# Hybrid attention block on one core: last value tiles and lambda moved, weight differences on VectorE, row scalings placed behind sums

## The chip, the cores and the metric

The kernel runs on one core of one Trainium2 chip. A time is the device time of one execution in microseconds (us); the number for a kernel is the median of several executions. One execution is recorded by the hardware profiler, and every row of a profile below is from that one.

Engines have short names in the profile: PE is TensorE's matrix products and PEld its weight loads (which overlap products), DVE is VectorE, ACT is ScalarE, POOL is GpSimd, SP is SyncE, which here only issues transfers.

## The reference

One decoder block on a sequence of 1024 rows of width 1024, all in float32. Every product is kept near float32 accuracy by splitting operands, as told in the next section.

```
h    = rms_norm(x, g_pre)
proj = h @ w_in                       # qa ka va fa za | qb kb vb zb | gates
ya   = fox_attention(qa, ka, va, log_sigmoid(fa + b_forget)) * silu(za)  # 8 heads of 64
qd, kd = rope(qb), rope(kb)           # 4 heads, two maps (q1,k1), (q2,k2) each
lam  = exp(sum(lambda_q1*lambda_k1)) - exp(sum(lambda_q2*lambda_k2)) + lam_init
yb   = (softmax(q1 k1^T) - lam * softmax(q2 k2^T)) v     # causal
yb   = rms_norm(yb, g_subln) * (1 - lam_init) * silu(zb)
ga, gb = sigmoid(gates)
merged = ga * (ya @ w_branch[0]) + gb * (yb @ w_branch[1])
out  = x + rms_norm(merged @ w_out, g_post)
```

## The kernel before, in words

**Split operands.** A float32 operand is held as `hi`, its rounding to the type fp32r, and `lo`, the remainder. A product of two operands is three products on PE: hi by hi, hi by lo, lo by hi. So each operand costs a copy (`hi`, on ACT or GpSimd) and a subtraction (`lo`, mostly on VectorE). For projection weights `load_w` does that (L260 the load, L264 or L266 `hi`, L268 `lo`), in three rings of slots with the tags `wraw`, `whi`, `wlo` of the pool `wpool`, two slots each. A tile that takes a slot waits until all readers of the tile two before it in that ring are done, stores to memory among them.

**Value phase (to about 111 us).** `x_block` normalises 128 rows of x and transposes them on PE (`xt`) into `hT`. `v_block(i)`, for eight row blocks, multiplies them with the value weights (`pv`, L197), splits the result into `vbs{i}` (values of the differential heads) and `vas{i}` (those of the forgetting heads), which are stored to memory as `vb_d` and `va_d` on SP's queue (L205, L213). `vbs` lies in the ring `whi`, `vas` in the ring `wlo`: the rings that `load_w` uses for the first keys' and queries' weights afterwards. Between blocks `h_combinations(k)` makes the sums of blocks of `hT` that the gates need later and stores them (`t_d`), through the four slots of the ring `wvraw` of the pool `xp`.

**Units 0 to 7 (about 111 to 582 us).** Units 0 to 3 are the differential heads, 4 to 7 pairs of forgetting heads. For each: keys and queries are projected (`pk`, `pq`, L278), in units 0 to 3 rotated: ACT copies the projection (`rawk`, L315), four transfers on SP bring its quarters into swapped order (`swk`, L319), VectorE multiplies by the cosines (L321), GpSimd the swapped tile by the sines (L322), VectorE adds (L323). Then come logits (`Sd`, `Sf`), softmax, and the products with the values. Lambda (`nlam`) is computed ahead of unit 0, in a tile `lt` of the pool of the softmax tiles: four small loads on SP (L588), two products (L591) and two sums (L593) on VectorE, an exponential on ACT, two small operations on VectorE (L596, L597).

**Gates (about 582 to 739 us) and branches (739 to 826 us).** The gate products and, at the end, the output products run by a scheme of seven products of half blocks instead of eight (`wino`, L728 the sums of its results on VectorE, L735 its products on PE, `x1` to `x7`). Its left operands are made in `left_operands`: sums `S1` to `S4` of blocks (L699), split into `a1` to `a7` (L686 `hi` on ACT, L687 `lo` on VectorE or GpSimd). In the branch stage, `branch` multiplies with `w_branch` (`pb`, L869), and `merge` multiplies by the stored gate on VectorE (L882, straight from PSUM, which frees the bank for PE; there are eight) and, for the second branch, adds to the merged tile `mg` on GpSimd (L884).

**Output weights.** Beside the branch products the seven right operands of the output products are made from the four blocks of `w_out`: `wo_sub` (L917) makes differences of 128x1024 on GpSimd, in place; `wo_parts` splits them (L910 on ACT, L911 on VectorE). The last of them and the first output operands are made side by side at about 826 to 840 us.

**Output (about 826 us to the end).** Four pairs of row blocks (i, i+4), named `o0` to `o3`, with seven products of 12 matmuls each. When the sum of a half row is done, `out_half` squares it on ACT (L965) and multiplies it by the output norm's weights (L968); when both halves of a row are there, ACT adds the two sums of squares (`ors`, L980) and GpSimd takes the power (L981). `row_out` then scales the two halves and adds the residual x (L997) and stores them. The residual loads (L947) go into columns of `mg` that are no longer needed. A generator step of `wino` is one product with its sums; `advance` runs one step, then issues the `row_out` that became ready in the step before:

```
        due = waiting[:]
        waiting.clear()
        next(gen, None)
        for f in due:
            f()
```

**What sets the order.** The program is written in one sequence; a scheduler with a simulated timeline then sets the order in which each engine's instructions stand, by its own costs and by when tiles come free. A changed dependence in one place can so change the order elsewhere. On each engine and each queue, instructions run strictly in that order. `tc.issue_after(ins)` tells the scheduler to place what is issued within it behind `ins`.

Of the kernel before, what the change touches and what calls it, by code (L numbers as in the profile page):

```python
# [16 lines left out]
P = 128  # L17
# [30 lines left out]
def tile_hybrid_block(  # L48
# [72 lines left out]
    with ExitStack() as st:  # L121
# [63 lines left out]
        def v_block(i):  # L185
            sl = slice(i * P, (i + 1) * P)
            hs = slice(i % 4 * P, (i % 4 + 1) * P)
            chunks = ((0, 512), (512, 768), (768, 1032))
            ps = [
                pv1.tile([P, CH], F32, tag=f"v{n}", name=f"pv{i}_{n}")[:, 0:b - a]  # L190
                for n, (a, b) in enumerate(chunks)
            ]
            for n, (a, b) in enumerate(chunks):
                first = True
                for k in range(KT):
                    for hp, wt in ((0, wv_hi), (0, wv_lo), (1, wv_hi)):
                        nc.tensor.matmul(  # L197
                            ps[n], lhsT=hT[hp][k // 4][i // 4][:, k % 4, hs], rhs=wt[k][:, a:b],
                            start=first, stop=(k == KT - 1 and hp == 1))
                        first = False  # L200
            sb = wpool.tile([P, 4, 256], F32R, tag="whi", name=f"vbs{i}")
            p0 = ps[0].rearrange("p (h c) -> p h c", h=4)
            nc.scalar.copy(sb[:, :, 0:128], p0)
            nc.vector.tensor_tensor(sb[:, :, 128:256], p0, sb[:, :, 0:128], op=ALU.subtract)
            nc.sync.dma_start(vb_d[sl], f32(sb))  # L205
            sa = wpool.tile([P, 8, 128], F32R, tag="wlo", name=f"vas{i}")
            for n, hh in ((1, 0), (2, 4)):
                pa = ps[n][:, 0:256].rearrange("p (h c) -> p h c", h=4)
                nc.scalar.copy(sa[:, hh:hh + 4, 0:64], pa)
                nc.vector.tensor_tensor(  # L210
                    sa[:, hh:hh + 4, 64:128], pa, sa[:, hh:hh + 4, 0:64], op=ALU.subtract)
            nc.vector.tensor_tensor(fg[:, i, :], ps[2][:, 256:264], bf_bc, op=ALU.add)
            nc.sync.dma_start(va_d[sl].rearrange("s a (b c) -> s (a b) c", b=2), f32(sa))  # L213

        def h_combinations(k):
# [24 lines left out]
            nc.vector.tensor_tensor(f21, f21, f11, op=ALU.subtract)  # L240
            parts(4, f21)

        x_block(0)
        for k in range(KT):
            load_wv(k)
# [3 lines left out]
        for i in range(NB):  # L249
            for j in XBLK[i]:  # L250
                x_block(j)
            v_block(i)
            for k in TBLK[i]:
                h_combinations(k)

# [27 lines left out]
    with ExitStack() as st:  # L283
# [299 lines left out]
            return load, load_v, groups  # L583


        lt = pp.tile([P, 4, 64], F32, tag="P", name="lt")
        for n, v in enumerate((lq1, lk1, lq2, lk2)):
            nc.sync.dma_start(lt[:, n, :], v[0:1].to_broadcast([P, 64]))  # L588
        le = small.tile([P, 2], F32, tag="le", name="le", bufs=1)
        for n in range(2):  # L590
            nc.vector.tensor_tensor(  # L591
                lt[:, 2 * n, :], lt[:, 2 * n, :], lt[:, 2 * n + 1, :], op=ALU.mult)
            nc.vector.tensor_reduce(  # L593
                out=le[:, n:n + 1], in_=lt[:, 2 * n, :], axis=mybir.AxisListType.X, op=ALU.add)
        nc.scalar.activation(le, le, AF.Exp)
        nc.vector.tensor_tensor(nlam, le[:, 1:2], le[:, 0:1], op=ALU.subtract)  # L596
        nc.vector.tensor_scalar(nlam, nlam, -LAM_INIT, None, op0=ALU.add)  # L597

        def forget_sums():

            fgf = fg.rearrange("p a b -> p (a b)")
# [89 lines left out]
    def left_operands(nm, a11, a12, a21, a22):  # L691
# [24 lines left out]
            return t  # L716
        return get

    def wino(nm, left, right, order, out11, out12, out21, out22):

        x, c = {}, {}
# [3 lines left out]
            return c[key]  # L725

        def add(dst, a, b):
            nc.vector.tensor_tensor(dst, a, b, op=ALU.add)  # L728

        for m in order:  # L730
            a = left(m)
# [142 lines left out]
    def merge(d, br, c, ps):  # L874
        sl = slice(c * CH, (c + 1) * CH)
        m = mg[:, d, sl]
        if br == 0:
            g = m
        else:
            g = tmp.tile([P, CH], F32, tag="t", name=f"gb{d}_{c}")  # L880
        nc.sync.dma_start(g, g_d[d][br][:, sl])
        nc.vector.tensor_tensor(g, ps, g, op=ALU.mult)  # L882
        if br == 1:
            nc.gpsimd.tensor_tensor(m, m, g, op=ALU.add)  # L884

    for br in range(2):
        for d in range(KT):
# [26 lines left out]
    def wo_sub(dst, a, b):  # L914
        for j in range(2):
            js = slice(2 * j, 2 * j + 2)
            nc.gpsimd.tensor_tensor(dst[:, js], a[:, js], b[:, js], op=ALU.subtract)  # L917

    wo_parts(1, r[1, 1], hslot[1, 1])
    wo_sub(r[1, 1], r[1, 2], r[1, 1])  # L920
# [26 lines left out]
        nc.sync.dma_start(xs, x2[i * P:(i + 1) * P, :].rearrange("p (k n) -> p k n", k=KT))  # L947
        xres[i] = xs

    waiting = []  # L950

    def advance(gen):

        due = waiting[:]
        waiting.clear()
        next(gen, None)
        for f in due:
            f()

    def out_half(i, e, o, st):  # L960

# [16 lines left out]
        if len(st) == 2:  # L978
            rs = small.tile([P, 1], F32, tag="ors", name=f"ors{i}")
            nc.scalar.activation(rs, ss, AF.Identity, bias=st[0][2])  # L980
            nc.gpsimd.tensor_tensor(rs, rs, mhalf[:, 0:1], op=ALU.pow)  # L981
            if i not in xres:
                residual(i, i)
            waiting.append(lambda: row_out(i, rs, st))

    def row_out(i, rs, st):
        for n, (e, o, _) in enumerate(st):
# [32 lines left out]
    for n, which in enumerate((0, 0, 0, 0, 0, 1, 0, 0, 1, 1, 1, 1, 1, 1)):  # L1020
        advance(pairs[which])
        if n == 0:
            for i in (3, 7):
                residual(i, i - 2)
    for f in waiting:
        f()
    xst.close()
    gw.close()
# [42 lines left out]
```

## Time and profile before

| what | us |
|---|---|
| median of three executions | 918.48 (919.04, 915.05, 918.48) |
| the profiled execution | 915.13 |
| its span, first to last instruction | 913.4 |
| PE busy | 885.6 (97%) |
| PE weight loads busy | 746.7 (82%) |
| VectorE busy | 604.2 (66%) |
| GpSimd busy | 468.5 (51%) |
| ScalarE busy | 440.5 (48%) |
| moved by DMA | 139.04 MB |

The mean granted clock of TensorE was 0.998 of full speed. A profile row that lists an instruction begins with its start and its duration in us, then the engine (SPq is SP's queue), the line of the kernel, the operation, output<-inputs without their numbers, the shapes, how many of them stand in the row, and in brackets how long the engine stood idle before it and what ended that idle time. A row of waits gives the instruction that waited, the one it waited for, and three numbers: us in total, times, the longest. A row of stretches gives the stretch, its length, the busy time of each engine and the count of its instructions, the granted clock, the DMA engines' busy share, and GB/s.

### The profile page before, as it was taken

To read this page: it belongs to the slowest core of one execution; us is meant where nothing else is said; L and a number is where in the kernel's file an instruction comes from. 1 tells how busy PE (TensorE), PEld (TensorE's weight loads), DVE (VectorE), ACT (ScalarE), POOL (GpSimd) and SP (SyncE) were. 2 spreads that over 40 slices of the span, in tenths; PEclk is the share of its full clock that TensorE was granted. 3 is DMA by queue.
4 is the path that set the end of the run, shared out by engine and by line. 5 is a ranking of instruction groups with operands and counts; after the bars stand their busy time and mean duration, and the time that the engine had idled before them with its cause. 6 is when DMAs were issued, how large, how long until landed. Compare 5 with 4: busy or idle time off the path is not lost. (4 is left out here: it accounts for less than half of the span.)

```text
span 913.4 us, 13656 instructions
## 1 busy us (share of the span) xinstructions
PE 885.6 (97%) x4600; PEld 746.7 (82%) x4600; DVE 604.2 (66%) x1123; ACT 440.5 (48%) x877; POOL 468.5 (51%) x439
## 2 busy tenths in 40 slices
PE   7999999999999999999999999999999999999996
PEld 5899978788888888888888888788888888887884
DVE  6757547878578574467648548425778893548996
ACT  3433225576657674365546648533443361313442
POOL 7325324545545456254434446417566526687861
PEclk9999999999999999999999999999999999999999
DMA  9556737434335260432523432596555498210395
GB/s 316 192 170 255 262 106 210 111 79 122 108 81 171 73 179 18 141 92 70 165 73 87 129 102 62 197 401 218 168 181 171 155 333 291 70 46 21 95 183 186
DMA packets 128648, 139.04 MB, mean 152 GB/s; under 512 B 10289, under 2 KB 96305, under 8 KB 127554
## 3 DMA queue, kind: packets, MB, share of 16 engines
q1 hardware_dynamic: 124210, 135.82, 47.4%
q0 software_dynamic: 4224, 2.10, 2.0%
q8 instruction: 36, 0.59, 0.3%
q14 instruction: 34, 0.28, 0.1%
q10 hardware_dynamic: 144, 0.26, 0.1%
HBM read 85.65 MB, written 37.81 MB: 135 GB/s over the span
## 5 line engine op out<-in xcount | busy, mean ns | idle before, releaser
L197 PE MATMUL pv<-wvhi,hT 128*128 128x264 f32 (+2 forms) x384 | 89.1, 324 | 0.4 <-DVE hT L183 0.4
L278 PE MATMUL pz<-hT,hi_z 128*128 128x512 f32 x256 | 83.3, 397 | 0.2 <-ACT sq L390 0.2
L278 PE MATMUL pk<-hT,hi_k 128*128 128x512 f32 x256 | 82.2, 395 | 0.9 <-DVE KB L331 0.9
L278 PE MATMUL pq<-hT,hi_q 128*128 128x512 f32 x256 | 81.7, 393 | 0.0
L735 PE MATMUL x_o<-wo_op,a_o 128*128 128x512 f32 x336 | 77.8, 392 | 1.1 <-ACT a_o L686 1.1
L869 PE MATMUL pb<-yT,hi_br 128*128 128x512 f32 x256 | 78.5, 389 | 0.0
L735 PE MATMUL x_g<-T,a_g 128*128 128x512 f32 x336 | 78.1, 391 | 0.0
L735 PEld LDWEIGHTS x_o<-wo_op,a_o 128*128 128x128 f32 x336 | 62.9, 188 | 15.8 <-ACT a_o L686 2.0
L735 PEld LDWEIGHTS x_g<-T,a_g 128*128 128x128 f32 x336 | 63.1, 188 | 13.9
L197 PEld LDWEIGHTS pv<-wvhi,hT 128*128 128x128 f32 x384 | 64.4, 190 | 6.1 <-DVE hT L183 0.7
L440 ACT ACTIVATE Pd<-Pd,mxd 128x128 f32<-128x128 f32 (+7 forms) x64 | 49.6, 775 | 35.4 <-DVE mxd L434 35.1
L553 POOL TENSOR_TENSOR cb<-cb,trim 128x128 f32<-128x128 f32 x64 | 30.3, 477 | 66.9 <-DVE mxf L434 44.1
L527 POOL TENSOR_SCALAR Pd<-Pd,l,nlam 128x128 f32<-128x128 f32 (+7 forms) x32 | 29.3, 915 | 65.6 <-DVE l L526 59.4
L197 PE MATMUL pv<-wvlo,hT 128*128 128x512 f32 (+2 forms) x192 | 62.1, 326 | 0.1
L558 POOL TENSOR_SCALAR Pf<-Pf,lf 128x1024 f32<-128x1024 f32 (+3 forms) x64 | 47.9, 753 | 27.7 <-DVE lf L557 24.7
L465 DVE TENSOR_TENSOR plf<-ptf,phf 128x512 fp32r<-128x512 f32 (+1 forms) x80 | 49.9, 635 | 18.0 <-ACT phf L464 17.2
L440 ACT ACTIVATE Pf<-Pf,mxf 128x1024 f32<-128x1024 f32 (+3 forms) x64 | 49.8, 777 | 20.6 <-DVE mxf L434 20.0
L735 PE MATMUL x_g<-hT,a_g 128*128 128x512 f32 x252 | 59.0, 391 | 0.0
L869 PEld LDWEIGHTS pb<-yT,hi_br 128*128 128x128 f32 x256 | 48.1, 188 | 9.9
L735 PEld LDWEIGHTS x_g<-hT,a_g 128*128 128x128 f32 x252 | 47.3, 188 | 10.4
L278 PEld LDWEIGHTS pk<-hT,hi_k 128*128 128x128 f32 x256 | 47.2, 188 | 10.3 <-DVE KB L331 1.5
L278 PEld LDWEIGHTS pq<-hT,hi_q 128*128 128x128 f32 x256 | 47.6, 188 | 9.2
(252 smaller groups left out, 2382.3 us busy)
## 6 DMA issues: line engine op xcount, KB each, us to landing
t_d<-t SPq DMA_DIRECT2D x16, 512.0 KB, 4.7
T<-t_d SPq DMA_DIRECT2D x8, 1024.0 KB, 17.8
raw<-in_w_in_dram SPq DMA_DIRECT2D x14, 512.0 KB, 5.5
vb_d<-vbs SPq DMA_DIRECT2D x8, 512.0 KB, 3.7
va_d<-vas SPq DMA_DIRECT2D x8, 512.0 KB, 3.1
raw_k<-in_w_in_dram SPq DMA_DIRECT2D x8, 512.0 KB, 5.0
raw_q<-in_w_in_dram SPq DMA_DIRECT2D x8, 512.0 KB, 4.4
V<-vb_d SPq DMA_DIRECT2D x4, 1024.0 KB
```

The costliest lines, as they stand in the source:

```text
L197: nc.tensor.matmul(ps[n], lhsT=hT[hp][k // 4][i // 4][:, k % 4, hs], rhs=wt[k][:, a:b], start=first, stop=(k == KT - 1 and hp == 1))
L278: nc.tensor.matmul(ps, lhsT=a[:, k, :], rhs=hT[h][k // 4][c][:, k % 4, :], start=(k == 0 and a is hi and h == 0), stop=(k == KT - 1 and a ...
L440: nc.scalar.activation(pr[:, 0:n], pr[:, 0:n], AF.Exp, bias=mx[:, len(pcs) - 1:len(pcs)], scale=-1.0, accum_out=le)
L465: nc.vector.tensor_tensor(pl[:, 0:n], pt[:, 0:n], ph[:, 0:n], op=ALU.subtract)
L527: nc.gpsimd.tensor_scalar(p2[:, 0:n], p2[:, 0:n], l2, nlam, op0=ALU.mult, op1=ALU.mult)
L553: nc.gpsimd.tensor_tensor(diag, diag, trim, op=ALU.add)
L558: nc.gpsimd.tensor_scalar(p1[:, 0:n], p1[:, 0:n], l1, 1.0, op0=ALU.mult, op1=ALU.mult)
L735: nc.tensor.matmul(x[m], lhsT=a[:, ai, k, :], rhs=right[m][bi][k], start=(k == 0 and n == 0), stop=(k == 3 and n == 2))
L869: nc.tensor.matmul(ps, lhsT=a[:, kk, :], rhs=yT[g][h][:, k % 2, sl], start=(k == 0 and a is hi and h == 0), stop=(k == 3 and a is lo))
```

## The change

Four edits; the arithmetic stays what it was.

- The value tiles of the last row block, `vbs7` and `vas7`, are taken from the ring `wvraw` of the pool `xp` (four slots) and not from `whi` and `wlo`.
- Lambda is computed in a function `lambdas()` that is called behind the third value block (i = 2) and not ahead of unit 0; its tile `lt` now comes from the ring `wlo`.
- `wo_sub` runs on VectorE and not on GpSimd, and so do the two last sums of `merge` (those of d = 7).
- `advance` holds each `row_out` for a number of steps (two for row 6, one for the others) and issues it behind the last sum made so far, by explicit order.

```diff
@@ -198,12 +198,15 @@
                             ps[n], lhsT=hT[hp][k // 4][i // 4][:, k % 4, hs], rhs=wt[k][:, a:b],
                             start=first, stop=(k == KT - 1 and hp == 1))
                         first = False
-            sb = wpool.tile([P, 4, 256], F32R, tag="whi", name=f"vbs{i}")
+            last = i == NB - 1
+            sb = (xp.tile([P, 4, 256], F32R, tag="wvraw", name=f"vbs{i}", bufs=4) if last
+                  else wpool.tile([P, 4, 256], F32R, tag="whi", name=f"vbs{i}"))
             p0 = ps[0].rearrange("p (h c) -> p h c", h=4)
             nc.scalar.copy(sb[:, :, 0:128], p0)
             nc.vector.tensor_tensor(sb[:, :, 128:256], p0, sb[:, :, 0:128], op=ALU.subtract)
             nc.sync.dma_start(vb_d[sl], f32(sb))
-            sa = wpool.tile([P, 8, 128], F32R, tag="wlo", name=f"vas{i}")
+            sa = (xp.tile([P, 8, 128], F32R, tag="wvraw", name=f"vas{i}", bufs=4) if last
+                  else wpool.tile([P, 8, 128], F32R, tag="wlo", name=f"vas{i}"))
             for n, hh in ((1, 0), (2, 4)):
                 pa = ps[n][:, 0:256].rearrange("p (h c) -> p h c", h=4)
                 nc.scalar.copy(sa[:, hh:hh + 4, 0:64], pa)
@@ -240,6 +243,21 @@
             nc.vector.tensor_tensor(f21, f21, f11, op=ALU.subtract)
             parts(4, f21)
 
+        def lambdas():
+
+            lt = wpool.tile([P, 4, 64], F32, tag="wlo", name="lt")
+            for n, v in enumerate((lq1, lk1, lq2, lk2)):
+                nc.sync.dma_start(lt[:, n, :], v[0:1].to_broadcast([P, 64]))
+            le = small.tile([P, 2], F32, tag="le", name="le", bufs=1)
+            for n in range(2):
+                nc.vector.tensor_tensor(
+                    lt[:, 2 * n, :], lt[:, 2 * n, :], lt[:, 2 * n + 1, :], op=ALU.mult)
+                nc.vector.tensor_reduce(
+                    out=le[:, n:n + 1], in_=lt[:, 2 * n, :], axis=mybir.AxisListType.X, op=ALU.add)
+            nc.scalar.activation(le, le, AF.Exp)
+            nc.vector.tensor_tensor(nlam, le[:, 1:2], le[:, 0:1], op=ALU.subtract)
+            nc.vector.tensor_scalar(nlam, nlam, -LAM_INIT, None, op0=ALU.add)
+
         x_block(0)
         for k in range(KT):
             load_wv(k)
@@ -250,6 +268,8 @@
             for j in XBLK[i]:
                 x_block(j)
             v_block(i)
+            if i == 2:
+                lambdas()
             for k in TBLK[i]:
                 h_combinations(k)
 
@@ -582,19 +602,6 @@
                                 u == 7 and g in FING)))
             return load, load_v, groups
 
-
-        lt = pp.tile([P, 4, 64], F32, tag="P", name="lt")
-        for n, v in enumerate((lq1, lk1, lq2, lk2)):
-            nc.sync.dma_start(lt[:, n, :], v[0:1].to_broadcast([P, 64]))
-        le = small.tile([P, 2], F32, tag="le", name="le", bufs=1)
-        for n in range(2):
-            nc.vector.tensor_tensor(
-                lt[:, 2 * n, :], lt[:, 2 * n, :], lt[:, 2 * n + 1, :], op=ALU.mult)
-            nc.vector.tensor_reduce(
-                out=le[:, n:n + 1], in_=lt[:, 2 * n, :], axis=mybir.AxisListType.X, op=ALU.add)
-        nc.scalar.activation(le, le, AF.Exp)
-        nc.vector.tensor_tensor(nlam, le[:, 1:2], le[:, 0:1], op=ALU.subtract)
-        nc.vector.tensor_scalar(nlam, nlam, -LAM_INIT, None, op0=ALU.add)
 
         def forget_sums():
 
@@ -716,6 +723,8 @@
             return t
         return get
 
+    sums = [None]
+
     def wino(nm, left, right, order, out11, out12, out21, out22):
 
         x, c = {}, {}
@@ -725,7 +734,7 @@
             return c[key]
 
         def add(dst, a, b):
-            nc.vector.tensor_tensor(dst, a, b, op=ALU.add)
+            sums[0] = nc.vector.tensor_tensor(dst, a, b, op=ALU.add).ins
 
         for m in order:
             a = left(m)
@@ -881,7 +890,8 @@
         nc.sync.dma_start(g, g_d[d][br][:, sl])
         nc.vector.tensor_tensor(g, ps, g, op=ALU.mult)
         if br == 1:
-            nc.gpsimd.tensor_tensor(m, m, g, op=ALU.add)
+            eng = nc.vector if d == KT - 1 else nc.gpsimd
+            eng.tensor_tensor(m, m, g, op=ALU.add)
 
     for br in range(2):
         for d in range(KT):
@@ -914,7 +924,7 @@
     def wo_sub(dst, a, b):
         for j in range(2):
             js = slice(2 * j, 2 * j + 2)
-            nc.gpsimd.tensor_tensor(dst[:, js], a[:, js], b[:, js], op=ALU.subtract)
+            nc.vector.tensor_tensor(dst[:, js], a[:, js], b[:, js], op=ALU.subtract)
 
     wo_parts(1, r[1, 1], hslot[1, 1])
     wo_sub(r[1, 1], r[1, 2], r[1, 1])
@@ -947,15 +957,15 @@
         nc.sync.dma_start(xs, x2[i * P:(i + 1) * P, :].rearrange("p (k n) -> p k n", k=KT))
         xres[i] = xs
 
-    waiting = []
+    waiting, step = [], [0]
 
     def advance(gen):
 
-        due = waiting[:]
-        waiting.clear()
+        step[0] += 1
         next(gen, None)
-        for f in due:
-            f()
+        while waiting and waiting[0][0] <= step[0]:
+            with tc.issue_after(sums[0]):
+                waiting.pop(0)[1]()
 
     def out_half(i, e, o, st):
 
@@ -981,7 +991,7 @@
             nc.gpsimd.tensor_tensor(rs, rs, mhalf[:, 0:1], op=ALU.pow)
             if i not in xres:
                 residual(i, i)
-            waiting.append(lambda: row_out(i, rs, st))
+            waiting.append((step[0] + (2 if i == 6 else 1), lambda: row_out(i, rs, st)))
 
     def row_out(i, rs, st):
         for n, (e, o, _) in enumerate(st):
@@ -1022,7 +1032,7 @@
         if n == 0:
             for i in (3, 7):
                 residual(i, i - 2)
-    for f in waiting:
+    for _, f in waiting:
         f()
     xst.close()
     gw.close()
```

How the order moves, at three places. Names in the rows are tiles with their serial numbers. The first place is VectorE at the end of the value phase; `lo_k0` and `lo_q0` are the remainders of the first keys' and queries' weights, `t6_3` and `t4_3` those of the last stored combinations of `hT`, `fg` the forget gates. Before:

```order
L204 TENSOR_TENSOR vbs7_1214<-pv7_0_1139,vbs7_1214 128x4x128
L268 TENSOR_TENSOR lo_k0_1282<-raw_k0_1279,hi_k0_1281 128x1024
L591 TENSOR_TENSOR lt_1262<-lt_1262 128x64
L210 TENSOR_TENSOR vas7_1218<-pv7_1_1140,vas7_1218 128x4x64
L593 TENSOR_REDUCE le_1267<-lt_1262 128x1
L591 TENSOR_TENSOR lt_1262<-lt_1262 128x64
L593 TENSOR_REDUCE le_1267<-lt_1262 128x1
L210 TENSOR_TENSOR vas7_1218<-pv7_2_1141,vas7_1218 128x4x64
L212 TENSOR_TENSOR fg_86<-pv7_2_1141,bf_bc_83 128x8
L596 TENSOR_TENSOR nlam_85<-le_1267 128x1
L597 TENSOR_SCALAR nlam_85<-nlam_85 128x1
L268 TENSOR_TENSOR lo_q0_1328<-raw_q0_1325,hi_q0_1327 128x1024
```

With the change:

```order
L288 TENSOR_TENSOR lo_k0_1282<-raw_k0_1279,hi_k0_1281 128x1024
L213 TENSOR_TENSOR vas6_1119<-pv6_1_1041,vas6_1119 128x4x64
L230 TENSOR_TENSOR t6_3_1142<-fa_3_1126,t6_3_1142 128x512
L213 TENSOR_TENSOR vas6_1119<-pv6_2_1042,vas6_1119 128x4x64
L215 TENSOR_TENSOR fg_86<-pv6_2_1042,bf_bc_83 128x8
L230 TENSOR_TENSOR t4_3_1148<-fb_3_1127,t4_3_1148 128x512
L206 TENSOR_TENSOR vbs7_1227<-pv7_0_1152,vbs7_1227 128x4x128
L288 TENSOR_TENSOR lo_q0_1328<-raw_q0_1325,hi_q0_1327 128x1024
L213 TENSOR_TENSOR vas7_1231<-pv7_1_1153,vas7_1231 128x4x64
L213 TENSOR_TENSOR vas7_1231<-pv7_2_1154,vas7_1231 128x4x64
L215 TENSOR_TENSOR fg_86<-pv7_2_1154,bf_bc_83 128x8
```

`lo_q0` now stands ahead of the two remainders of `vas7` and not behind them, `lo_k0` ahead of those of `vas6`, and lambda's operations are gone from here.

The second place is VectorE at the change from the branch stage to the output products; `wo_op61` and `wo_op41` are remainders of output weights, `wo11` and `wo21` the blocks in which the differences are made, `a5_o0` and `a6_o0` remainders of left operands of the first output pair. Before:

```order
L882 TENSOR_TENSOR gb7_1_8642<-pb7_1_1_8629,gb7_1_8642 128x512
L911 TENSOR_TENSOR wo_op61_8679<-wo11_8646,wo_op60_8678 128x1024
L911 TENSOR_TENSOR wo_op41_8687<-wo11_8646,wo_op40_8686 128x1024
L699 TENSOR_TENSOR S1_o0_8780<-mg_8053 128x512
L699 TENSOR_TENSOR S2_o0_8782<-S1_o0_8780,mg_8053 128x512
L699 TENSOR_TENSOR S1_o1_8802<-mg_8053 128x512
L687 TENSOR_TENSOR a5_o0_8824<-S1_o0_8780,a5_o0_8824 128x512
L699 TENSOR_TENSOR S2_o1_8804<-S1_o1_8802,mg_8053 128x512
L911 TENSOR_TENSOR wo_op41_8687<-wo11_8646,wo_op40_8686 128x1024
L687 TENSOR_TENSOR a6_o0_8784<-S2_o0_8782,a6_o0_8784 128x512
```

With the change:

```order
L921 TENSOR_TENSOR wo_op61_8679<-wo11_8646,wo_op60_8678 128x1024
L927 TENSOR_TENSOR wo11_8646<-wo21_8652,wo11_8646 128x1024
L894 TENSOR_TENSOR mg_8053<-mg_8053,gb7_1_8642 128x512
L927 TENSOR_TENSOR wo11_8646<-wo21_8652,wo11_8646 128x1024
L706 TENSOR_TENSOR S1_o0_8780<-mg_8053 128x512
L921 TENSOR_TENSOR wo_op41_8687<-wo11_8646,wo_op40_8686 128x1024
L706 TENSOR_TENSOR S2_o0_8782<-S1_o0_8780,mg_8053 128x512
L706 TENSOR_TENSOR S1_o1_8802<-mg_8053 128x512
L921 TENSOR_TENSOR wo_op41_8687<-wo11_8646,wo_op40_8686 128x1024
L694 TENSOR_TENSOR a5_o0_8824<-S1_o0_8780,a5_o0_8824 128x512
L706 TENSOR_TENSOR S2_o1_8804<-S1_o1_8802,mg_8053 128x512
L694 TENSOR_TENSOR a6_o0_8784<-S2_o0_8782,a6_o0_8784 128x512
```

The last two differences (L927) and the last merge sum (L894) now stand ahead of the sums `S1` and `S2`, and both `wo_op41` ahead of `a5_o0`. On PE, at the same place, the products of `x6_o0` and its neighbours stood so before:

```order
L735 MATMUL x7_o1_8767<-wo_op70_8664,a7_o1_8764 128x512
L735 MATMUL x6_o0_8787<-wo_op60_8678,a6_o0_8784 128x512
L735 MATMUL x6_o0_8787<-wo_op61_8679,a6_o0_8784 128x512
L735 MATMUL x6_o1_8809<-wo_op60_8678,a6_o1_8806 128x512
L735 MATMUL x6_o1_8809<-wo_op61_8679,a6_o1_8806 128x512
L735 MATMUL x5_o0_8827<-wo_op50_8670,a5_o0_8824 128x512
L735 MATMUL x5_o0_8827<-wo_op51_8671,a5_o0_8824 128x512
```

With the change:

```order
L744 MATMUL x7_o1_8767<-wo_op70_8664,a7_o1_8764 128x512
L744 MATMUL x6_o0_8787<-wo_op60_8678,a6_o0_8784 128x512
L744 MATMUL x6_o0_8787<-wo_op61_8679,a6_o0_8784 128x512
L744 MATMUL x6_o0_8787<-wo_op60_8678,a6_o0_8784 128x512 x2
L744 MATMUL x6_o0_8787<-wo_op61_8679,a6_o0_8784 128x512
...
L744 MATMUL x6_o0_8787<-wo_op60_8678,a6_o0_8784 128x512
L744 MATMUL x6_o1_8809<-wo_op60_8678,a6_o1_8806 128x512
L744 MATMUL x6_o1_8809<-wo_op61_8679,a6_o1_8806 128x512
L744 MATMUL x5_o0_8827<-wo_op50_8670,a5_o0_8824 128x512
```

All twelve products of `x6_o0` now follow each other; before, those of two more products stood behind its first two, and its last ten behind `x4_o0`'s first.

The third place is VectorE at the end; `c12_o3` and `c11_o3` are the sums for row 3, `go7` and `go3` rows 7 and 3. Before:

```order
L728 TENSOR_TENSOR cu2_o3_9226<-x4_o3_9279,cu2_o3_9226 128x512
L968 TENSOR_TENSOR go7_0_9295<-cu2_o3_9226,gx_8705 128x512
L997 SCALAR_TENSOR_TENSOR go7_1_9273<-go7_1_9273,ors7_9297,mg_8053 128x512
L997 SCALAR_TENSOR_TENSOR go7_0_9295<-go7_0_9295,ors7_9297,mg_8053 128x512
L728 TENSOR_TENSOR c12_o3_9248<-x3_o3_9305,c12_o3_9248 128x512
L968 TENSOR_TENSOR go3_1_9321<-c12_o3_9248,gx_8705 128x512
L728 TENSOR_TENSOR c11_o3_9150<-x2_o3_9331,c11_o3_9150 128x512
```

With the change:

```order
L737 TENSOR_TENSOR cu2_o3_9226<-x4_o3_9279,cu2_o3_9226 128x512
L978 TENSOR_TENSOR go7_0_9295<-cu2_o3_9226,gx_8705 128x512
L737 TENSOR_TENSOR c12_o3_9244<-x3_o3_9305,c12_o3_9244 128x512
L1007 SCALAR_TENSOR_TENSOR go7_1_9273<-go7_1_9273,ors7_9297,mg_8053 128x512
L1007 SCALAR_TENSOR_TENSOR go7_0_9295<-go7_0_9295,ors7_9297,mg_8053 128x512
L978 TENSOR_TENSOR go3_1_9321<-c12_o3_9244,gx_8705 128x512
L737 TENSOR_TENSOR c11_o3_9150<-x2_o3_9331,c11_o3_9150 128x512
```

The sum `c12_o3` moved ahead of the two scalings of row 7.

## The prediction, made before the changed kernel was run

> **What bounds the kernel now.** I read the page's busy shares first, then what TensorE (PE) waits for, then the stretches round those waits.
>
> ```profile
> PE 885.6 (97%) x4600; PEld 746.7 (82%) x4600; DVE 604.2 (66%) x1123; ACT 440.5 (48%) x877; POOL 468.5 (51%) x439
> ```
>
> PE is busy for 885.6 of 913.4 us, so what can be saved without taking products away is the 28 us in which it stands still. Its waits name part of them:
>
> ```profile
> PE Sd L432 <- DVE mxd L434: 3.2, 5, 1.2
> PE pq L278 <- DVE lo_q L268: 1.8, 1, 1.8
> PE x_o L735 <- ACT a_o L686: 1.1, 2, 0.8
> ```
>
> The change reaches two of them: `pq` waiting for the first query weights' remainder `lo_q`, and `x_o`, the output products, waiting for an operand. (The three numbers are us in total, times, longest.) The third place is the stretch behind PE's last product, where the end hangs on one engine after the other; its rows stand in part C.
>
> **Part A: last value block's tiles and lambda, near 110 to 119 us.**
>
> ```profile
> 116.57 0.61 PE L278 MATMUL pq<-hT,hi_q 128*128 128x512 f32 x2
> 119.00 0.50 PE L278 MATMUL pq<-hT,lo_q 128*128 128x512 f32 x1 [1.81 <-DVE lo_q L268]
> 119.33 0.62 PE L278 MATMUL pq<-hT,hi_q 128*128 128x512 f32 x2
> 120.03 0.62 PE L278 MATMUL pq<-hT,hi_q 128*128 128x512 f32 x2
> 104.09 0.58 SPq L213 DMA_DIRECT2D va_d<-vas  x1
> 115.00 0.33 SPq L213 DMA_DIRECT2D va_d<-vas  x1
> 117.72 1.23 DVE L268 TENSOR_TENSOR lo_q<-raw_q,hi_q 128x1024 fp32r<-128x1024 f32 x1 [2.41 <-DMA va_d<-vas]
> 116.77 0.59 ACT L315 COPY rawk<-pk 128x512 f32<-128x512 f32 x1 [1.88 <-PE pk L278]
> 118.97 0.38 SPq L260 DMA_DIRECT2D raw_q<-in_w_in_dram  x1
> 119.44 2.51 SPq L319 DMA_DIRECT2D swk<-rawk  x4
> ```
>
> `lo_q` takes the slot of the last value tile, so it waits until that tile's store, issued at 115.00, has landed at 117.72, 2.7 us later. With the last value tiles in slots of their own, `lo_q` takes the slot of the block before, whose store goes out near 104 us. SP now puts one weight load (0.4 us) and one transfer ahead of it; at two to three times the 2.7 us it lands by about 113. One remainder of 1.23 us then ends by 114.5, over 2 us before PE asks at 117.0. In triples of 0.70 us (119.33 to 120.03) the second triple of `pq` would begin at 116.57 + 0.70 = 117.27 instead of 119.33: **2.06 us** less. The rotation of the keys must follow, or the gain stops there: its four copies stand on SP behind `raw_q` (118.97), which waits for `lo_q`; that load goes out earlier now, so they start once ACT's key copy is ready, at 117.4, also 2.0 us sooner. Bounds: 0, if unit 0 gives it back (a rival), to 2.06. I take 2.06, because products, copies and rotation move together and the orders behind are the same rows.
>
> Queued on VectorE behind `lo_q`'s wait are now the last value tile's remainders, whose store, by the code, nobody reads before unit 4, and the first product of the keys' rotation, which needs PE's key products; ACT copies those at 116.77, so it cannot start sooner anyway.
>
> Lambda's two products and sums leave this place (0.22 us each) and go behind the third value block, where VectorE now waits for their loads:
>
> ```profile
> L178 PE MATMUL xt<-ident,xg x40: 270/272/273, 35.1 to 57.6; 128*128 128x128 f32 x40
> 48.40 0.33 SPq L205 DMA_DIRECT2D vb_d<-vbs  x1
> 52.67 0.69 DVE L183 TENSOR_TENSOR hT<-xt,hT 128x512 fp32r<-128x512 f32 x1 [0.30 <-ACT hT L182]
> 106.83 1.18 SPq L588 DMA_DIRECT2D lt<-in_lambda_k_dram  x1
> 111.31 0.22 DVE L591 TENSOR_TENSOR lt<-lt 128x64 f32<-128x64 f32 x1 [1.43 <-DMA lt<-in_lambda_k_dram]
> ```
>
> The loads go out behind 48.7; two issues of about 1.1 us, then 4.5 us from issue to use (106.83 to 111.31), make the first pair usable near 54.3. Behind it on VectorE stands the remainder of the seventh transposed block (52.67 now, then about 54.7); the last transposes, at about 57.3, need its PSUM tile. Cover: 57.3 − 55.4 = 1.9 us. Cost taken: 0; without the cover, one us per us.
>
> **Part B: output weights on VectorE, 765 to 846 us.** Eight differences of 128x1024 leave GpSimd, and two of sixteen merge sums.
>
> ```profile
> 765.38 9.47 POOL L917 TENSOR_TENSOR wo<-wo,wo 128x1024 f32<-128x1024 f32 x4 [1.25 <-issue]
> 763.50 0.69 DVE L882 TENSOR_TENSOR mg<-pb,mg 128x512 f32<-128x512 f32 x1 [2.03 <-PE pb L869]
> 760.00:800.00 40.00, 40.00 (x178) 33.12 (x177) 17.35 (x19) 9.91 (x10) 29.98 (x14) 1.00 0.46 150
> ```
>
> (In the last row: the stretch, its length, then the busy us and count of PE, PEld, VectorE, ACT and GpSimd, the granted clock, the DMA share, GB/s.) On VectorE eight at 1.23 us (its 128x1024 row below) and two at 0.69 are 11.2 us. Six lie before 800 us. The first now waits on VectorE for its load, which GpSimd had at 765.3 (765.38 less its own issue): VectorE gets there after the merge product of 763.50, at 764.2, and waits about 1.1 us. The merge products queued behind it free PSUM banks; PE fills one in 2.7 us (its merge rows stand 2.03 idle and 0.69 busy apart) and has eight, and VectorE is busy for 17.35 of these 40 us. So the six cost 0; without the spare banks they would cost up to 1.1 + 4 × 1.23 = 6.0. The last two stand on the path of the first output products:
>
> ```profile
> 825.86 11.21 PE L735 MATMUL x_o<-wo_op,a_o 128*128 128x512 f32 x48
> 837.85 0.73 PE L735 MATMUL x_o<-wo_op,a_o 128*128 128x512 f32 x2 [0.78 <-ACT a_o L686]
> 838.89 7.38 PE L735 MATMUL x_o<-wo_op,a_o 128*128 128x512 f32 x31 [0.31 <-ACT a_o L686]
> 825.78 1.23 DVE L911 TENSOR_TENSOR wo_op<-wo,wo_op 128x1024 fp32r<-128x1024 f32 x1 [1.75 <-ACT wo_op L910]
> 826.92 0.69 DVE L882 TENSOR_TENSOR gb<-pb,gb 128x512 f32<-128x512 f32 x1
> 827.52 5.29 DVE L911 TENSOR_TENSOR wo_op<-wo,wo_op 128x1024 fp32r<-128x1024 f32 x2
> 832.73 2.88 DVE L699 TENSOR_TENSOR S_o<-mg 128x512 f32<-128x512 f32 x1
> 831.69 3.37 POOL L917 TENSOR_TENSOR wo<-wo,wo 128x1024 f32<-128x1024 f32 x1
> 837.69 1.59 POOL L699 TENSOR_TENSOR S_o<-mg,S_o 128x512 f32<-128x512 f32 x1 [2.63 <-DVE a_o L687]
> ```
>
> Products follow each other by 0.23 us (10.82 over 47), so the 51st would start at 825.86 + 50 × 0.23 = 837.4; it started at 838.9: **1.5 us lost** today. Where the two engines overlap, VectorE's S_o needed 2.88 us and ended 0.55 behind GpSimd's 835.06: one works at a time. [...]
>
> The 51st product was the first of x6_o1; it is now the third of x6_o0, which needs the remainder of a6_o0 from VectorE. From 826.92 on there stand ahead of that remainder five operations of 128x1024 (1.14 from start to start, 825.78 to 826.92) and seven of 128x512 (0.60, 826.92 to 827.52): 5.7 + 4.2 = 9.9, so it starts at 836.8. If it runs at once it is done at 837.5, a loss of 0.2; behind GpSimd's S4 sum (about 1.15 without a lock) at 838.6, a loss of 1.3. The next such remainder, a6_o1, is asked for 32 products later, at 846.0, and comes by 842 free or, with four more locks of 1.2 us, at 846.5: another 0.5. So after: 0.2 to 1.8 lost, against 1.5. S4 waits for a5_o0's remainder today (837.69, `a_o`), two operations ahead of a6_o0's in the new order, so I take the first lock as striking and leave the four out: 1.3, that is **−0.2** (bounds −1.3 to +0.3).
>
> **Part C: order behind the last sums.**
>
> ```profile
> 899.82 4.96 PE L735 MATMUL x_o<-wo_op,a_o 128*128 128x512 f32 x21
> 903.52 1.42 DVE L997 SCALAR_TENSOR_TENSOR go<-go,ors,mg 128x512 f32<-128x512 f32 x2 [1.08 <-DMA out_dram<-cu_o]
> 904.85 0.68 DVE L728 TENSOR_TENSOR c_o<-x_o,c_o 128x512 f32<-128x512 f32 x1
> 905.57 0.69 DVE L968 TENSOR_TENSOR go<-c_o,gx 128x512 f32<-128x512 f32 x1
> 906.18 0.68 DVE L728 TENSOR_TENSOR c_o<-x_o,c_o 128x512 f32<-128x512 f32 x1
> ```
>
> PE ends at 904.78, but the last sum starts at 906.18, behind row 7's two scalings, the sum of x3_o3, and a product. The last twelve of the 21 products are x2_o3's, so x3_o3 was complete near 902.1, and its sum of 0.68 fits the gap of 1.08 before 903.52.
>
> With the change that sum stands ahead of the scalings. That alone frees 0.72 us (904.85 to 905.57). [...] What follows (square, power, scaling, store) is unchanged. Bounds 0 to 1.23; I take **−1.2**, since row 7's scalings need to come only 0.5 us sooner for it.
>
> Sum: −2.06 − 0.2 − 1.2 = −3.5 us. The profiled execution took 915.13 (span 913.4), near the fastest of 915.05 to 919.04; from the median 918.48 that gives **915.0**, from its own time 911.6.
>
> **Rivals.** *The output stage sheds its whole wait*: no lock strikes, B −1.3: 913.9. For it, GpSimd is idle once its last merge is gone; against it, S4 starts just before a6_o0.
> *Unit 0 gives A back*: then −1.4, 917.1.
>
> ```profile
> 160.00:180.00 20.00, 17.79 (x90) 14.14 (x89) 17.74 (x31) 10.95 (x21) 12.33 (x9) 1.00 0.48 119
> ```
>
> For it, VectorE is busy for 17.74 of 20 us there; against it, its chain starts 2 us sooner too.
> *The tail waits for a transfer*: the last residual load, C 0: 916.2.
>
> ```profile
> DMA to landing us min/median/max: 6.7/6.8/7.0
> 897.02 0.56 SPq L947 DMA_DIRECT2D mg<-in_x_dram  x1
> ```
>
> *Lambda's loads are late, slower*: VectorE stands before lt in the value phase. If the first pair lands after 59.6 (57.3 − 1.2 + 3.5), the kernel is slower; at the 17.8 us of the slowest kind it lands at 67.7, PE loses 11.6, and the time is 926.6.
>
> ```profile
> T<-t_d SPq DMA_DIRECT2D x8, 1024.0 KB, 17.8
> ```
>
> Against it: those are 1 MB loads in a crowd; 50 to 60 us moves little.
> *It doesn't do what it says*: lo_q0 waits as long for the earlier store; 917.1 as well.
>
> **How the numbers follow.** Forecast 0.50, whole wait shed 0.17, A given back 0.15, tail hidden 0.10, lambda late 0.05, store no earlier 0.03. A measurement of this kernel tells 0.5% (4.6 us) from no change: 913.9 is just that edge. Faster: half of the 0.17 and, with run spread of 2 us, a fifth of the 0.50: 0.19. Slower: most of lambda's 0.05: 0.04. Same: 0.77. Range 911.5 (all gains from a fast run's level) to 918.3 (A and most of C gone).
>
> **What would show it.** A: no wait of pq for lo_q, and lo_q ending before 115. B: x_o's waits naming a remainder on DVE, 0.2 to 1.8 us. C: PE's end to the last sum under 0.3 us. Wrong if PE shows a new wait at xt near 57 us, if the Sd waits grow by 2 us, or if the last scaling waits for a load.

## The result, and the profile after

Twelve executions of the changed kernel have a median of 910.88 us (909.96 to 914.84), twelve of the kernel before, beside them, one of 917.40 (915.05 to 921.10). The ratio on record, which is not the quotient of these two medians (0.9929), is **0.9942, 95% interval 0.9927 to 0.9957**: 0.58% faster. That is clear of zero, but the interval reaches both sides of the 0.5% that the prediction took as its edge, so whether the gain passes it is not decided. Applied to the 918.48 known before, the ratio gives 913.2, where 915.0 was forecast with a range of 911.5 to 918.3; the median itself lies 0.6 below that range. The profiled execution took 909.96 us with a span of 908.15, against 915.13 and 913.36.

Where did the 5.2 us of span go? Both kernels run the same 4600 products on PE. The table takes the start of the k-th product in either execution and shows how the lead of the changed kernel grew from one k to the next; the tail is the span less PE's end.

| stretch | products | change, us | forecast |
|---|---|---|---|
| start, value phase | up to 600 | -0.39 | 0 |
| A: first keys and queries | 600 to 750 | -2.11 | -2.06 |
| units 0 to 7 | 750 to 3200 | -0.04 | 0 |
| gates, branches | 3200 to 4290 | 0.00 | 0 |
| B: first output products | 4290 to 4400 | -1.31 | -0.2 |
| rest of the output products | 4400 to 4600 | 0.00 | 0 |
| tail after PE | | -1.37 (8.59 to 7.22) | -1.2 |

A in the timeline of PE, VectorE and SP after: `pq` follows `pk` with no wait, `lo_q` ends at 113.4, and the last value store goes out behind it.

```profile
116.19 0.62 PE L298 MATMUL pq<-hT,hi_q 128*128 128x512 f32 x2
116.64 0.39 PE L298 MATMUL pq<-hT,lo_q 128*128 128x512 f32 x1
116.86 0.62 PE L298 MATMUL pq<-hT,hi_q 128*128 128x512 f32 x2
112.19 1.23 DVE L288 TENSOR_TENSOR lo_q<-raw_q,hi_q 128x1024 fp32r<-128x1024 f32 x1 [5.00 <-DMA va_d<-vas]
105.19 0.56 SPq L216 DMA_DIRECT2D va_d<-vas  x1
114.11 0.35 SPq L216 DMA_DIRECT2D va_d<-vas  x1
117.00 2.52 SPq L339 DMA_DIRECT2D swk<-rawk  x4
54.99 0.23 DVE L253 TENSOR_TENSOR lt<-lt 128x64 f32<-128x64 f32 x1 [0.46 <-DMA lt<-in_lambda_k_dram]
57.10 0.60 PE L178 MATMUL xt<-ident,xg 128*128 128x128 f32 x4
```

The store ahead (105.19) took 6.9 us to land, in time all the same. Lambda's products ended at 55.2; the transposes at 57.10 did not wait. B and the tail after:

```profile
823.33 22.95 PE L744 MATMUL x_o<-wo_op,a_o 128*128 128x512 f32 x98
834.27 1.29 DVE L694 TENSOR_TENSOR a_o<-S_o,a_o 128x512 fp32r<-128x512 f32 x2
833.90 5.70 POOL L706 TENSOR_TENSOR S_o<-mg,S_o 128x512 f32<-128x512 f32 x1 [13.76 <-DVE a_o L694]
883.62 17.30 PE L744 MATMUL x_o<-wo_op,a_o 128*128 128x512 f32 x75
898.22 0.69 DVE L737 TENSOR_TENSOR c_o<-x_o,c_o 128x512 f32<-128x512 f32 x1 [1.31 <-PE x_o L744]
898.83 1.41 DVE L1007 SCALAR_TENSOR_TENSOR go<-go,ors,mg 128x512 f32<-128x512 f32 x2
900.96 0.69 DVE L737 TENSOR_TENSOR c_o<-x_o,c_o 128x512 f32<-128x512 f32 x1
```

98 output products run without a gap, where 48 did before. The remainder of a6_o0 is the first of the two at 834.27: with the lead of 2.54 us that is 836.8 in the time of before, to the tenth the start that the prediction worked out. But S4 did not strike it. GpSimd's sum was ready at 833.90 and lasted 5.70 us, against 1.3 alone (the merge sums): VectorE finished the operation it was at and ran five more first, all on SBUF alone, and S4 ended 1.17 us after the last of them. In the tail, the last sum starts 0.03 us after PE's end (900.93), not 1.41.

### The profile page after: what moved, and what is told of

Its sections match the earlier page's. It is cut to its first block, busy times and chain, and to the rows that moved or that the text cites. A ratio compares the mean times of both kernels' runs of the same rounds, so it can differ in the third digit from the quotient of the medians.

```text
span 908.1 us, 13652 instructions
## 1 busy us (share of the span) xinstructions
PE 884.7 (97%) x4600; PEld 746.4 (82%) x4600; DVE 606.3 (67%) x1133; ACT 441.6 (49%) x877; POOL 447.2 (49%) x429
## 4 chain that ended last, share of the span: by engine, by line
PE 82%; DVE 6%; issue 4%; POOL 3%; DMA 2%; ACT 2%; SPq 1%; POOLq 0%; DVEq 0%; ACTq 0%
PE x_g L744 15%; PE pb L878 10%; PE pv L197 9%; PE x_o L744 9%; PE pz L298 8%; PE pk L298 7%; PE pq L298 7%; PE ypf L505 3%; PE ptf L481 2%; PE pg L298 2%; PE ypd L505 2%; PE Sd L452 2%; PE ptd L481 1%; PE Sf L452 1%; PE Sd L453 1%
```

## The experiments

**Each part alone, and A with B.** The edits are those of the change, split; all the rest is the kernel before.

```diff
 A only:  vbs7, vas7 in "wvraw"; lambdas() called behind v_block(2)
 B only:  wo_sub and the merge sums of d = 7 on nc.vector
 C only:  advance() with step counts and tc.issue_after(sums[0])
 A and B: the change without the lines of C
```

> Only part A: the last value tiles in the four-slot ring and lambda behind the third value block; output weights and row scalings as before. Theory 1 (the three parts act each at its own place and add up): PE gains 2.1 us between its products 600 and 700 and keeps it to the end, the 51st output product still starts 1.5 us late, PE's end to the kernel's end stays at 8.6 us; about -2.1 us, ratio 0.998. Rival (the parts need each other, or the units give A back): less than 1 us of it is left at PE's last product.

> Only part B: the eight differences of the output weights and the last two merge sums on VectorE; the rest as before. Theory 1: PE's output products run without a gap, -1.3 us between PE's products 4300 and 4400 and nothing elsewhere, ratio 0.9985. Prediction's own size for B (GpSimd's sum S4 strikes VectorE ahead of a6_o0's remainder): -0.2 us, and a wait of PE of 1.1 us or more at the third product of x6_o0. Rival (B's gain came only with A's and C's other order): no change.

> Only part C: row scalings by explicit order behind the sums; the rest as before. Theory 1: from PE's end to the kernel's end 7.2 us in place of 8.6, PE itself unchanged, -1.4 us, ratio 0.9985. Rival (the tail is short only because VectorE was less loaded with B in): 8.3 us or more.

> The changed kernel without part C (row scalings issued as before). Its order differs from the changed kernel's on VectorE's last rows alone: three sums stand behind scalings again, the sum of x3_o3 behind row 7's among them. Prediction's theory (C's order shortens the tail by 1.2 us): PE's end to the kernel's end is 8.3 us or more, and the kernel 1.2 us slower than the changed one. Rival, from the run with B alone, whose tail was 7.2 us with the old order (B takes the backlog off VectorE, so the chain of rows 6 and 7 comes 2 us sooner against PE, and the order no longer matters): 7.2 us, the changed kernel's time within 0.3 us.

| kernel | ratio, interval | A | units | B | tail |
|---|---|---|---|---|---|
| the change | 0.9942 (0.9927 to 0.9957) | -2.11 | -0.04 | -1.31 | 7.22 |
| A only | 0.9962 (0.9944 to 0.9979) | -2.11 | +3.05 | +0.03 | 8.62 |
| B only | 0.9947 (0.9927 to 0.9967) | -0.06 | -0.08 | -1.27 | 7.23 |
| C only | 0.9984 (0.9966 to 1.0002) | -0.16 | -0.46 | +0.03 | 7.24 |
| A and B | 0.9959 (0.9945 to 0.9973) | -2.11 | +1.24 | -1.31 | 7.23 |

A and B act at their own places, as expected, and B at the tail besides. **C does not add up with them**: alone it shortens the tail to 7.24 us, B alone shortens it as much (7.23) with the old order, and with B in, C has 0.01 left to give. This rests on the traced tails; the times of the change and of A and B (0.9942 and 0.9959) have intervals that overlap. The +3.05 of A only belongs to its profiled execution, the slowest of its twelve (916.18, median 913.96): PE lost it in pieces of 0.3 to 1.0 between 136 and 167 us, and six other executions with all of A show -0.52 to +2.83 there, four further ones without it -0.46 to +0.10. Of that +2.83 (the tiny sum, below), 2.3 lie at 286 to 300 us, where its granted clock falls for a while (0.71 at 294 to 298 us). That A brings these losses on is possible, and the times, a gain of 0.38%, speak against a regular one; it was not settled.

How B shortens the tail stands in VectorE's rows. Sum of x6_o3 and the last scalings and sums, first in the kernel before, then with B only:

```profile
894.68 0.69 DVE L728 TENSOR_TENSOR cu_o<-x_o,c_o 128x512 f32<-128x512 f32 x1
```

```profile
891.38 0.68 DVE L728 TENSOR_TENSOR cu_o<-x_o,c_o 128x512 f32<-128x512 f32 x1
900.59 1.41 DVE L998 SCALAR_TENSOR_TENSOR go<-go,ors,mg 128x512 f32<-128x512 f32 x2 [1.09 <-POOL ors L982]
901.92 0.68 DVE L728 TENSOR_TENSOR c_o<-x_o,c_o 128x512 f32<-128x512 f32 x1
903.55 0.69 DVE L728 TENSOR_TENSOR c_o<-x_o,c_o 128x512 f32<-128x512 f32 x1 [0.23 <-PE x_o L735]
```

Before, that sum stands 10.1 us ahead of PE's end (904.77), with B only 12.1 us (903.52). The same two us separate the two kernels on all but one of VectorE's rows from about 34 to 6 us ahead of PE's end: VectorE was behind since the output weights were made, and never caught up. Rid of that backlog, row 7's scalings (900.59) and the sum behind them (901.92) are over before x2_o3 is complete, and the last sum waits for PE (0.23), whatever the order.

**A in halves.**

```diff
 tiles only:   sb, sa of the last block from xp, tag "wvraw"; lambda as before
 lambda only:  lambdas() behind v_block(2); sb, sa from wpool as before
```

> Of part A only the value tiles in the four-slot ring; lambda stays ahead of unit 0, its loads now behind the last value store on SP. Theory (the store's landing is what the first query weights' remainder waits for): no wait of pq for lo_q, -2.1 us between PE's products 600 and 750, nothing at the output products. Rival (lambda's late products on VectorE are what holds it): the wait stays above 1 us.

> Of part A only lambda's move; the value tiles stay in the weights' rings, so lo_q still waits for the last value store to land. From the rows of before: without lambda's products, which wait for their loads (2.17 us at 114.17), the last value tile's remainder ends near 111.7, its store goes out near 111.8 and lands 2.7 us later at 114.5, and lo_q ends near 115.7, 1.3 us before PE asks. Theory now (either half of A is enough): -2.1 us, as with the tiles alone. The prediction's reading (the slots are what counts): the wait stays, shortened at most by a us.

Lambda alone gave the whole -2.11 (span 911.5). Its rows of SP and VectorE:

```profile
112.33 0.32 SPq L213 DMA_DIRECT2D va_d<-vas  x1
115.50 1.23 DVE L285 TENSOR_TENSOR lo_q<-raw_q,hi_q 128x1024 fp32r<-128x1024 f32 x1 [3.13 <-DMA va_d<-vas]
```

The store still holds `lo_q` back, but it goes out 2.7 us sooner than at 115.00, and `lo_q` is done by 116.7 (115.7 was expected), before PE wants it. The tiles alone **lost 2.48 us** at this place (span 915.8). Rows of PE and SP:

```profile
124.90 0.79 PE L281 MATMUL pk<-hT,hi_k 128*128 128x512 f32 x2 [2.70 <-DVE rotk L324]
114.93 0.35 SPq L216 DMA_DIRECT2D va_d<-vas  x1
120.35 0.33 SPq L591 DMA_DIRECT2D lt<-in_lambda_q_dram  x1
122.21 2.50 SPq L322 DMA_DIRECT2D swk<-rawk  x4
```

`pq` no longer waits, but lambda's loads now stand on SP behind the last value store and ahead of the keys' four copies. The first of them waits until that store has landed and goes out only at 120.35, the copies at 122.21 (117.00 with the change), and PE waits for the rotated keys. The theory's number for the tiles was wrong in its sign.

**B in halves, and who gets the turn.** First the differences without the two merge sums:

```diff
 merge(): nc.gpsimd.tensor_tensor(m, m, g)      as before
 wo_sub(): nc.vector.tensor_tensor(dst, a, b)   as in the change
```

> Of part B only the eight differences on VectorE; the last two merge sums stay on GpSimd; nothing of A and C. If the differences carry B: PE's output products run without a gap and the tail is 7.2 us, a span near that of B alone (910.7 us). If the sums matter (the last one falls into VectorE's row, one turn of 1.1 us, and S1 waits for it): PE waits 1 to 2 us at the output products.

PE's waits at the output products, the first of them at the third product of x6_o0:

```profile
838.62 11.30 PE L735 MATMUL x_o<-wo_op,a_o 128*128 128x512 f32 x48 [0.53 <-DVE a_o L687]
850.66 11.66 PE L735 MATMUL x_o<-wo_op,a_o 128*128 128x512 f32 x49 [0.73 <-POOL a_o L687]
```

Together they are 1.3 us, within what was expected if the sums matter, and B's term came to +0.26, not -1.27. The last merge sum on GpSimd (828.25, 2.21 us) cost VectorE one turn. So this term needs both halves; the tail was 7.23 us and needs the differences alone.

Then three kernels with sums added on GpSimd, and one with a copy on VectorE (`dmy` is a tile that nobody reads). In each the order on PE and VectorE up to a6_o0's remainder is that of the change. Where the expectations speak of ports or a strike, what the trace of before shows is one of the two engines waiting for the other: a 128x512 sum on VectorE took 2.88 us beside GpSimd's last difference (832.73), the next one 0.69 (835.65). What they contend for, no run shows.

```diff
 four sums: + for _ in range(4): nc.gpsimd.tensor_tensor(dmy, mg[:, 7, 0:512], mg[:, 7, 512:1024], ...)
 one sum:   + nc.gpsimd.tensor_tensor(dmy, mg[:, 7, 0:512], mg[:, 7, 512:1024], ...)
 tiny sum:  + nc.gpsimd.tensor_tensor(dmy[:, 0:8], mg[:, 7, 0:8], mg[:, 7, 512:520], ...)
 copy:      + nc.vector.tensor_copy(dmy, x7_o0[:, 0:256])    behind a6_o0's remainder
```

> The changed kernel with four sums of 128x512 added on GpSimd, whose result nobody reads; they become ready when VectorE has written the last merge sum, near 828 us, just as VectorE begins its row of operations that ends in the remainder of a6_o0. The order on PE and VectorE is the same as in the changed kernel. Prediction's theory (the two engines take turns, each strike costs VectorE 1.15 us): the remainder comes 3.5 to 4.6 us later and PE waits about as long at the third product of x6_o0; the kernel gets 3.3 to 4.6 us longer. Rival (VectorE keeps the ports as long as its operations follow each other without a gap, GpSimd starves): GpSimd's first sum lasts to about 838 us, PE waits for nothing new there, and the time is that of the changed kernel, at most 1 us more through a later S4.

> As the run with four added sums of 128x512 on GpSimd, with one. Theory (each operation of GpSimd that falls into VectorE's row costs it one turn of 1.1 to 1.2 us, S4 included once GpSimd is awake): two turns, 2.2 us at a6_o0's remainder, of which PE shows about 2.1. Rival (S4 is kept out by VectorE's row): one turn, 1.1 us. If the price were not one turn per operation, the four sums' 6.1 us would not come down to a third.

> The changed kernel with one sum of 128x8 added on GpSimd, whose result nobody reads; it becomes ready with VectorE's last merge sum, near 828 us, 5 us ahead of the sum S4 of the first pair. The order on the other engines is the same. Theory (the strike that the prediction priced at 1.15 us is real, and S4 missed it only because GpSimd came out of 14 us of standing still): S4 lasts 1.6 to 1.8 us as behind the four sums, a6_o0's remainder ends 1.1 us later, PE waits about 1 us at the third product of x6_o0, and the kernel gets 0.5 to 1.5 us longer for a sum that itself takes a tenth of a us. Rival (VectorE's closed row keeps S4 out, whatever GpSimd did before): S4 lasts 5.7 us again and PE waits for nothing.

> The changed kernel with one copy of 128x256 from PSUM added on VectorE, right behind a6_o0's remainder, whose result nobody reads; it doesn't delay that remainder. Question: what keeps GpSimd's sum S4 out for 4.5 us while VectorE runs six operations. If it is VectorE's closed row of operations on SBUF alone: S4 starts at the copy and lasts 2.2 to 2.8 us. If it is a delay of GpSimd's own (a fixed 5.7 us): 5.7 us again. If it lasts 6.0 to 6.1 us, up to the end of VectorE's row, which the copy moves by 0.3, plus 1.16: S4 is kept out for the whole row, copy or not. PE waits for nothing at the output products in any of them, up to x6_o1.

| kernel | PE's wait at x6_o0 | B's term | S4 lasts |
|---|---|---|---|
| the change | none | -1.31 | 5.70 |
| four sums | 4.25 and 0.95 | +6.07 | 1.65 |
| one sum | 2.19 | +2.46 | 1.59 |
| tiny sum | 1.12 | -0.13 | 1.61 |
| copy | none | -1.30 | 2.22 |

With four sums VectorE and GpSimd take turns. VectorE's rows (its 128x512 takes 0.68 alone) and GpSimd's:

```profile
830.28 1.79 DVE L706 TENSOR_TENSOR S_o<-mg 128x512 f32<-128x512 f32 x1
832.00 2.32 DVE L921 TENSOR_TENSOR wo_op<-wo,wo_op 128x1024 fp32r<-128x1024 f32 x1
834.24 1.78 DVE L706 TENSOR_TENSOR S_o<-S_o,mg 128x512 f32<-128x512 f32 x1
835.94 1.75 DVE L706 TENSOR_TENSOR S_o<-mg 128x512 f32<-128x512 f32 x1
829.31 7.83 POOL L1025 TENSOR_TENSOR dmy<-mg 128x512 bf16<-128x512 f32 x4 [7.88 <-DVE mg L894]
```

Each sum costs VectorE one turn of 1.1 us (1.79 less 0.68), so the theory of turns holds, and the rival that VectorE always shuts GpSimd out falls. The time came out longer than these waits: B's term rose by 7.4 us with four sums (3.3 to 4.6 were said) and by 3.8 with one, where PE waited 5.2 and 2.2. The granted clock fell there, to 0.50 and 0.71 in a stretch of 4 us, as told at the end. With the tiny sum the strike that the prediction had priced comes about. GpSimd, VectorE and PE:

```profile
837.47 1.61 POOL L706 TENSOR_TENSOR S_o<-mg,S_o 128x512 f32<-128x512 f32 x1 [4.76 <-DVE a_o L694]
837.86 3.47 DVE L694 TENSOR_TENSOR a_o<-S_o,a_o 128x512 fp32r<-128x512 f32 x2
839.68 3.49 PE L744 MATMUL x_o<-wo_op,a_o 128*128 128x512 f32 x14 [1.12 <-DVE a_o L694]
```

S4 gets its turn at once, the two remainders take 3.47 us and not 1.29, and PE waits 1.12 us: for a sum of eight columns, most of B is gone at this place. That sum itself stands at 1.12 us in the trace (831.59), not at the tenth that was expected. With the copy from PSUM added instead, S4 slips in during it:

```profile
834.76 0.42 DVE L744 COPY dmy<-x_o 128x256 f32<-128x256 f32 x1
833.79 2.22 POOL L707 TENSOR_TENSOR S_o<-mg,S_o 128x512 f32<-128x512 f32 x1 [13.76 <-DVE a_o L694]
```

So it was VectorE's closed row of operations on SBUF alone that kept S4 out in the change, not a delay of GpSimd's own. Why a GpSimd operation sometimes gets the next turn against such a row and sometimes waits for its end stays open. The 5.7 us came back in all four executions that have this row and no added work (the change, B only, A and B, the differences alone), after GpSimd had been idle for 7.0 to 13.8 us; S4 got its turn at once after 2.4 to 4.8 us of idleness, but the added sums did so after 7.9, so the idleness alone does not decide.

**The kernel before again.**

> The kernel before once more, for a second profiled execution. Theory (the terms are properties of the order, not of one execution): pq waits 1.8 us for lo_q, the 51st output product starts 1.5 us late, PE's end to the kernel's end is 8.6 us; what differs from the first execution lies in the units and at the start, up to 3 us in all.

`pq` waited 1.91 us, the tail was 8.59 us, B's term +0.03: all as in the first execution. But A's stretch was 1.73 us longer still, and only 0.1 of that is the wait. The stretches of before in the first and then in this execution; the third number from the end is the granted clock:

```profile
120.00:124.00 4.00, 4.00 (x19) 3.29 (x18) 0.00 (x0) 0.00 (x0) 0.00 (x0) 1.00 0.78 197
```

```profile
120.00:124.00 4.00, 4.00 (x13) 3.17 (x13) 0.28 (x1) 0.00 (x0) 0.00 (x0) 0.66 0.75 191
```

After its wait PE got 13 products through in 4 us and not 19. The expectation had left this out.

## Why the prediction came out as it did

The direction was right, and the forecast of -3.5 us came out at -5.2 in the profiled pair. "Within 0.5%" was given 0.77 and "faster" 0.19; the 0.58% lies just past that edge, with an interval that reaches back over it. Of the 1.7 us beyond the forecast, 1.1 are B's at PE, 0.2 the tail's and 0.4 the start's.

- **A, right in size (-2.06; measured -2.11), half right in its reason.** `lo_q` ended at 113.4 (by 114.5 was said), the rotation moved along, the units gave nothing back in this execution, and lambda's cover held (first pair at 53.45; 54.3 was said). But the step "with the last value tiles in slots of their own" was not what the gain needed: lambda's move alone brings it, and the slots alone cost 2.48 us. The prediction read the wait of `lo_q` for the store and did not ask why the store was late. The row that tells it is VectorE's second lambda product, which waited for its load ahead of the value remainders:

```profile
114.17 0.23 DVE L591 TENSOR_TENSOR lt<-lt 128x64 f32<-128x64 f32 x1 [2.17 <-DMA lt<-in_lambda_k_dram]
```

- **B, mis-sized: "I take the first lock as striking: 1.3, that is -0.2"; measured -1.31**, the other end of the bounds (-1.3). The price of a strike was right (1.12 us with the tiny sum), the time of the remainder was right, and the six early differences cost 0 as said; the strike did not come. The rival "the output stage sheds its whole wait", given 0.17, is what happened; its reason (GpSimd idle) was not: GpSimd was ready, and was kept out. Struck each time, B would have been at the other bound, +0.3; with the four sums VectorE's 128x512 sums on SBUF took 1.75 to 1.79 us where GpSimd got a turn (0.68 without), and in the row that mattered after the change it got none.
- **B's second gain was missing from the sum.** Work taken off the two engines at 826 to 846 us was costed only where PE waits at once. VectorE stayed 2.05 us behind to the end, and the tail is where that is paid.
- **C, right in size for the wrong edit (-1.2; tail -1.37).** The step "That alone frees 0.72 us" and the bound of 1.23 were worked out on the trace of before, as if B were not in. Alone C gives 1.35, beside B 0.01: that the size came out is luck. The 1.23 has the last sum start 0.17 us behind PE's end, which no run shows; it started 0.03 behind it, so the bound was low by 0.14.
- **The rest**: -0.39 us at the start, where the executions of one kernel differ by as much (+0.64 in the second of before).
- **A rival was missing**: a wait of PE can cost more than its length, through the clock: 1.6 us more in the second execution of the kernel before. It may be part of why the medians lie 6.5 us apart and the profiled executions 5.2, but no run here settles that. Of 23 further executions of the kernel before on one chip, the five with a mean clock of 0.998 average 915.8 us and the ten at 0.996 and less 918.4; of 11 on another, the seven at 0.998 average 915.7 and the two at 0.996 914.8. Nor does the mean clock tell whether the clock fell within the kernel: one sum and tiny sum, where it did, and A only, where it did not, all have 0.997.

## What to carry to other kernels

Ask of a late operand what made its releaser late, and of a moved transfer what stands behind it on its queue: here four small loads were worth 2.1 us by the products that wait for them in VectorE's order, and 2.5 by their place on SP's queue. When several edits meet in one chain, cost them one after the other, each on the timeline that the earlier ones leave; gains that look separate (B's backlog, C's order) can be the same 1.4 us. Where two engines take turns, as VectorE and GpSimd did here (1.79 us for a sum that takes 0.68 alone), a term can have two values, and a harmless added instruction can flip it (B's from -1.31 to -0.13 with the tiny sum): keep both ends in the range and look in the trace at which one came.

## What the runs showed of the hardware

**TensorE's granted clock fell behind some short waits, as far as 0.50.** After PE's waits of 1.91 (kernel before, second execution), 2.19 (one sum), 2.70 (tiles only) and 4.25 us (four sums) the granted clock fell to 0.50 to 0.71 in a stretch of 4 us; after 1.81 (before, first execution), 1.79 (differences alone), 1.76 (B only), 1.66 (C only) and 1.12 us (tiny sum) it did not (1.00). The length of the wait alone does not decide: with the tiny sum the clock fell behind a wait of 0.94 us (294.51) that follows one of 0.48 (293.19), and the kernel before has one of 0.91 us at this place without a fall. The stretches of the tiny sum and then of before:

```profile
294.00:298.00 4.00, 3.06 (x11) 2.29 (x10) 3.39 (x10) 3.92 (x12) 1.51 (x2) 0.71 0.29 66
```

```profile
294.00:298.00 4.00, 3.09 (x18) 2.56 (x17) 3.88 (x13) 3.53 (x10) 1.53 (x2) 1.00 0.29 65
```

In four of these five falls two stretches in a row are together 1.7 us short of the full clock, worked out from their means (0.66 and 0.92 in the second execution of before: 0.34 and 0.08 of 4 us); with the four sums three are 3.4 us short (0.89, 0.50, 0.76). Behind them the clock is at 1.00 again. Rows of PE with the tiles only, after the wait of 2.70:

```profile
125.48 0.63 PE L281 MATMUL pk<-hT,lo_k 128*128 128x512 f32 x1
125.91 1.05 PE L281 MATMUL pk<-hT,hi_k 128*128 128x512 f32 x2
126.76 0.63 PE L281 MATMUL pk<-hT,lo_k 128*128 128x512 f32 x1
```

Products follow each other by 0.43 us there and by 0.23 elsewhere. Why PE's wait of 1.81 us passes without a fall and one of 1.91 does not, no run here decides.

**The last sum follows PE's last product by 0.03 us** in the trace (900.96 after 900.93), which counts the modelled end of a product.
